# Cached keys turned in 32x32 squares: both attentions of the sample rows laid out anew

## The chip, the cores and the metric

One Trainium2 chip, one of its cores. The metric is the device time of one execution in microseconds. The engines that matter below: TensorE (PE; its weight load is shown apart as PEld), VectorE (DVE), ScalarE (ACT), GpSimd (POOL) and SyncE (SP), whose queue issues nearly all transfers between the chip's memory and the on-chip memory.

## The reference

One decoder layer runs over 512 prompt rows and over 32 sample rows (8 sequences of 4 new rows), all in fp32. The layer mixes an mLSTM and a differential attention, then attends to 256 memory tokens, then runs a gated feed-forward network. Only two parts for the sample rows matter here.

Differential attention over a paged cache: 8 sequences, 2 pages of 128 rows each, 4 heads, each head with two components of 64 numbers:

```python
past_k = cache_dk[l][page_table].reshape(Bs, past_len, DA_HEADS, 2, DA_QK_DIM)
s = einsum('bqhcd,bkhcd->bhcqk', q, k) * DA_QK_DIM ** -0.5   # k: 256 cached rows and the 4 new ones
p = softmax(where(mask, s, -inf))
a = p[:, :, 0] - lam * p[:, :, 1]
out = einsum('bhqk,bkhd->bqhd', a, v)
```

Attention to cached memory tokens: 8 sequences, 256 tokens, 4 heads of 256 numbers:

```python
s = einsum('bqhd,bkhd->bhqk', q, mk) * MEM_HEAD_DIM ** -0.5
o = einsum('bhqk,bkhd->bqhd', softmax(s), mv)
```

The keys of both caches lie in memory with the rows (tokens) outermost, while a score is a sum over the numbers of a head; so the keys have to be turned before TensorE, which sums over partitions, can use them.

## The kernel before

The program is one long function; instructions are recorded in program order, and a planner then orders them on each engine by simulated times and priorities. On each engine that order is fixed when the kernel runs. `burst` and `issue_after` keep groups of matmuls together. On-chip memory is divided into rings of tiles: six staging tiles of 1024 columns (`stage()`), four weight slots of 2048 (`wp`), eleven larger tiles (`S`), and banks of the accumulation memory (`mmp()`, five; `at()`, three). A tile's next use waits until its last user is done. Weights arrive in a staging tile, and Scalar and Vector split them into a high and a low part in a weight slot; three matmuls then make one fp32 product.

Paged attention (the loop over `pipe(NB, dk_load, dk_turn, dk_scores)`): `dk_load` gathers the two pages of a sequence into one staging tile, 128 rows on 128 partitions. `dk_turn` transposes each head's 128x128 square on TensorE (`tr`, L1225), and Scalar and Vector copy the results out of the accumulation memory into a weight slot (`kT`, L1226); GpSimd adds the four new rows (L1221). `dk_scores` multiplies them per head with queries in which the other component is zero (`qz`, L1238), two sequences at a time. Vector masks and takes the maximum, Scalar the exponential and its sum, for each sequence apart (`sample_exp`, L1055 and L1056). `sample_softmax` then scales, by matmuls with selecting coefficients (`csz`, L1075), so that both components are combined and all sequences stand in one tile, which two transposes and eight copies spread for the product with the values. In each step of this loop one step of the prompt's own attention (`next(prompt)`) and some leftover projections (`F.run`) are recorded, so that TensorE's work is mixed.

Memory attention: `mk_load` brings 128 tokens by 1024 numbers, `mk_turn` transposes eight squares on TensorE (L1476), copied out by Scalar and Vector (L1477); `mk_scores` does two matmuls for each head and sequence (L1484), then `sample_exp`; after all eight sequences `sample_softmax`, and `mv_out` sums the values (L1506). The loads begin before the second half of the query projection (`gemmB` over `hqT`, L485), the first four sequences are turned inside it, and the others between steps of the prompt's memory attention (`ch_soft`, `ch_turn`, `ch_out`). `mv_load` brings the values into staging tiles, weight slots and one S tile, as they come free. Output projection weights (`w_mo`) follow in the staging tiles.

Of the kernel before, what the change touches and what calls it, by code (L numbers as in the profile page):

```python
# [7 lines left out]
F32 = mybir.dt.float32  # L8
# [10 lines left out]
NB = 8  # L19
# [15 lines left out]
for _n, _w in (("ident", 128), ("cos", 40), ("sin", 40), ("nsin", 40), ("dmask", 8), ("cm4", 4), ("cA", 1), ("cB", 1),  # L35
               ("comb", 16), ("selD", 8), ("selX", 8), ("selB", 8), ("cmask", 128), ("maskT", 128), ("maskS", 32)):
    CONST_COLS[_n] = (_off, _w)
    _off += _w
# [39 lines left out]
def kernel(ctx: ExitStack, tc: tile.TileContext, I, O):  # L78
# [972 lines left out]
    csz = cst.tile([P, NB, NS], F32, name="csz")  # L1051
    nc.gpsimd.memset(csz, 0.0)

    def sample_exp(sall, b, ps, nm, su):
        VRED(out=nm[:, b:b + 1], in_=ps, axis=AX.X, op=MAX, negate=True)  # L1055
        ACT(out=sall[:, b, :], in_=ps, func=AF.Exp, bias=nm[:, b:b + 1], accum_out=su[:, b:b + 1])  # L1056

    def sample_softmax(sall, su, coef, sel, oname, between=None):


        cf = small(NB, "scf")
        nc.vector.reciprocal(out=cf, in_=su)
        if coef is not None:
            VTS(out=cf, in0=cf, scalar1=coef, scalar2=None, op0=MUL)
        VTT(out=cf, in0=cf, in1=sel, op=MUL)
        VTT(out=view(csz, 0, [(64, NB // 2), (48, 2), (1, 16)]),
            in0=con("comb").unsqueeze(1).unsqueeze(1).broadcast_to([P, NB // 2, 2, 16]),
            in1=cf.rearrange("p (i e) -> p i e", e=2).unsqueeze(3).broadcast_to([P, NB // 2, 2, 16]), op=MUL)
        az = S([P, 2, H, NB * NS], F32, oname + "z")
        nc.gpsimd.memset(az, 0.0)  # L1070
        w = sall.shape[2]
        pa = at("spa")
        for e in range(2):
            for i in range(NB // 2):
                mm(pa[NS * i:NS * i + NS, :w], lhsT=csz[:, 2 * i + e, :], rhs=sall[:, 2 * i + e, :], start=(e == 0), stop=(e == 1))  # L1075
        a = Z("spc")[:, :w]
        nc.scalar.copy(out=a, in_=pa[:, :w])
        behind = between() if between else None
# [8 lines left out]
        return a, [az[:, 0], az[:, 1]]  # L1087

    def gather(name, b, g, out):
        v = nc.sync.value_load(ptab[0:1, 2 * b + g:2 * b + g + 1], min_val=0, max_val=I[name].shape[1] - 1)  # L1090
        dma(out=out, in_=I[name][0, bass.ds(v, 1)].rearrange("n s h d -> (n s) (h d)"))
# [105 lines left out]
    qz = sm.tile([P, H, 2, 2, 16], F32, name="qz", tag="qz", bufs=1)  # L1197
    nc.gpsimd.memset(qz, 0.0)
    for c in range(2):
        rr = slice(64 * c, 64 * c + 64)  # L1200
        nc.gpsimd.tensor_copy(out=qz[rr, :, :, c, :], in_=dqT[rr, :, SEQ:].rearrange("p h (g r) -> p h g r", g=2))
# [9 lines left out]
    kst, kts, pts, aTs, outs, rcs = {}, {}, {}, {}, {}, {}  # L1211

    def dk_load(b):
        st = stage()
        kst[b] = [st[:, 0:512], st[:, 512:1024]]
        for g in range(2):
            gather("cache_dk", b, g, kst[b][g])

    def dk_turn(b):
        kt = kts[b] = wp.tile([P, H, 260], F32, name="kT", tag="W")  # L1220
        nc.gpsimd.tensor_copy(out=kt[:, :, 256:260], in_=dkT[:, :, SEQ + TS * b:SEQ + TS * (b + 1)])  # L1221
        for g in range(2):
            ps = at("tpk")
            for h in range(H):
                tr(ps[:, h * P:(h + 1) * P], kst[b][g][:, h * P:(h + 1) * P], ident)  # L1225
            (VCP if g else nc.scalar.copy)(out=kt[:, :, g * P:(g + 1) * P], in_=v2(ps, P))  # L1226

    def dk_scores(b):

        if b % 2 == 0:  # L1230
            return
        pair = {}
# [714 lines left out]
```

## Time and profile before

| | us |
|---|---|
| median of 3 runs | 949.08 |
| lowest, highest | 947.5, 950.35 |
| span of the profiled execution | 947.0 |

The profiled execution's own time is given by its span, from the first to the last instruction; the times of the runs lie some 0.5 to 3.4 us above it. The granted TensorE clock is full throughout (mean 0.995, lower only at the very end). The stretches named below: paged attention from about 245 to 286 us, memory attention from about 405 to 485 us of the span. The page gives busy time by engine; the stretches and the groups of instructions are answers to queries on the same trace. A row of the time line gives start and duration in us, engine, source line, operation and operands, and how many instructions are merged in it; a row of groups gives the form, the count, busy time, mean duration in ns, and the idle time of the engine before them.

### The profile page before, as it was taken

To read this page: it belongs to the slowest core of one execution; us is meant where nothing else is said; L and a number is where in the kernel's file an instruction comes from. 1 tells how busy PE (TensorE), PEld (TensorE's weight loads), DVE (VectorE), ACT (ScalarE), POOL (GpSimd) and SP (SyncE) were. 2 spreads that over 40 slices of the span, in tenths; PEclk is the share of its full clock that TensorE was granted. 3 is DMA by queue.
4 is the path that set the end of the run, shared out by engine and by line. 5 is a ranking of instruction groups with operands and counts; after the bars stand their busy time and mean duration, and the time that the engine had idled before them with its cause. 6 is when DMAs were issued, how large, how long until landed. Compare 5 with 4: busy or idle time off the path is not lost. (4 is left out here: it accounts for less than half of the span.)

```text
span 947.0 us, 17080 instructions
## 1 busy us (share of the span) xinstructions
PE 927.3 (98%) x6612; PEld 808.2 (85%) x6612; DVE 601.1 (63%) x1128; ACT 388.5 (41%) x750; POOL 195.9 (21%) x384
## 2 busy tenths in 40 slices
PE   8999999999999999999999999999999999999995
PEld 5899787889866778998777899989988998999974
DVE  6745145565887448735654778637757775676767
ACT  5655233344676457625544433322212222222232
POOL 6611000025432215300000554001110110110114
PEclk9999999999999999999999999999999999999998
DMA  8960023344870429946944732062043313512023
GB/s 273 301 197 7 1 89 137 89 123 139 270 265 7 165 97 340 297 155 211 358 167 135 209 122 80 26 179 67 17 133 108 94 27 96 149 49 90 24 92 117
DMA packets 120673, 130.27 MB, mean 138 GB/s; under 512 B 8567, under 2 KB 86232, under 8 KB 120592
## 3 DMA queue, kind: packets, MB, share of 16 engines
q1 hardware_dynamic: 114408, 125.69, 42.1%
q10 hardware_dynamic: 6184, 3.48, 1.2%
q8 instruction: 52, 0.85, 0.4%
q14 instruction: 29, 0.24, 0.1%
HBM read 112.22 MB, written 16.93 MB: 136 GB/s over the span
## 5 line engine op out<-in xcount | busy, mean ns | idle before, releaser
L485 PE MATMUL mm<-fT,wslot 128*128 128x256 f32 x1872 | 235.9, 288 | 0.0
L485 PEld LDWEIGHTS mm<-fT,wslot 128*128 128x128 f32 x1872 | 234.4, 188 | 1.8 <-issue 0.8
L146 ACT CAST wslot<-wst 128x1024 fp32r<-128x1024 f32 x125 | 130.8, 1050 | 251.3 <-issue 71.7
L147 DVE TENSOR_TENSOR wslot<-wst,wslot 128x1024 fp32r<-128x1024 f32 x125 | 155.1, 1245 | 81.3 <-ACT wslot L146 80.8
L1758 PE MATMUL mm<-wslot,act 128*128 128x512 f32 (+1 forms) x180 | 70.2, 391 | 0.0
L1759 PE MATMUL mm<-wslot,act 128*128 128x512 f32 (+1 forms) x180 | 70.0, 392 | 0.0
L1757 PE MATMUL mm<-wslot,act 128*128 128x512 f32 (+1 forms) x180 | 69.3, 387 | 0.0
L1663 POOL COPY cvo<-u 128x2 f32<-128x2 f32 x43 | 10.5, 243 | 203.6 <-DVE u L1661 193.5
L411 PE MATMUL mm<-wslot,hT 128*128 128x512 f32 x128 | 51.3, 402 | 0.0
L485 PE MATMUL mm<-hT,wslot 128*128 128x256 f32 (+1 forms) x384 | 51.0, 289 | 0.0
L413 PE MATMUL mm<-wslot,hT 128*128 128x512 f32 x128 | 51.0, 399 | 0.0
L412 PE MATMUL mm<-wslot,hT 128*128 128x512 f32 x128 | 50.8, 397 | 0.0
L1658 DVE TENSOR_TENSOR u<-mm,rsb 128x256 f32<-128x256 f32 x43 | 18.1, 424 | 50.0 <-PE mm L485 50.0
L485 PEld LDWEIGHTS mm<-hT,wslot 128*128 128x128 f32 x384 | 49.2, 188 | 0.5 <-issue 0.2
L1757 PEld LDWEIGHTS mm<-wslot,act 128*128 128x128 f32 x180 | 34.3, 191 | 8.0 <-issue 0.8
L1759 PEld LDWEIGHTS mm<-wslot,act 128*128 128x128 f32 x180 | 33.8, 188 | 7.3 <-issue 0.4
L1758 PEld LDWEIGHTS mm<-wslot,act 128*128 128x128 f32 x180 | 33.8, 188 | 7.2
L1675 ACT ACTIVATE c<-c 128x560 f32<-128x560 f32 x21 | 14.1, 672 | 56.7 <-DVE c L1669 56.7
L1669 DVE SCALAR_TENSOR_TENSOR c<-u,cvT,c 128x560 f32<-128x560 f32 x43 | 34.3, 797 | 0.9
L1668 DVE SCALAR_TENSOR_TENSOR c<-u,cvT,c 128x560 f32<-128x560 f32 x43 | 34.1, 793 | 0.2
L1770 DVE TENSOR_TENSOR yp<-mm,yp 128x512 f32<-128x512 f32 (+1 forms) x41 | 27.2, 673 | 5.2 <-PE mm L1759 5.1
L413 PEld LDWEIGHTS mm<-wslot,hT 128*128 128x128 f32 x128 | 24.1, 188 | 5.0
(476 smaller groups left out, 1850.8 us busy)
## 6 DMA issues: line engine op xcount, KB each, us to landing
wst<-in_w_up_dram SPq DMA_DIRECT2D x42, 512.0 KB
wst<-in_w_in_dram SPq DMA_DIRECT2D x28, 512.0 KB
wst<-in_w_down_dram SPq DMA_DIRECT2D x20, 512.0 KB
wst<-in_cache_mem_k_dram SPq DMA_DIRECT2D x16, 512.0 KB
vt<-in_cache_mem_v_dram SPq DMA_DIRECT2D x10, 512.0 KB
wst<-in_w_mk_dram SPq DMA_DIRECT2D x8, 512.0 KB
xb<-in_x_prompt_dram SPq DMA_DIRECT2D x8, 512.0 KB
wst<-in_cache_dk_dram SPq DMA_DIRECT2D x16, 256.0 KB
```

The lines of the kernel that those rows point to most:

```text
L146: nc.scalar.copy(out=hi, in_=src)
L147: (eng or nc.vector).tensor_tensor(out=lo, in0=src, in1=f32(hi), op=SUB)
L411: mm(ps[b], lhsT=xt.hi(k, c0, c0 + n), rhs=s[:, 0, kk, :], start=(k == 0), stop=False)
L412: mm(ps[b], lhsT=xt.hi(k, c0, c0 + n), rhs=s[:, 1, kk, :], start=False, stop=False)
L413: return mm(ps[b], lhsT=xt.lo(k, c0, c0 + n), rhs=s[:, 0, kk, :], start=False, stop=(k == nk - 1))
L485: mm(ps[i], lhsT=s[:, l, k, :], rhs=x(k, c0, c1), start=(k == 0 and j == 0), stop=(k == 7 and j == 2))
L1668: STT(out=c, in0=u[:, 1:EXT - 1], scalar=w[1], in1=c, op0=MUL, op1=ADD)
L1669: STT(out=c, in0=u[:, 0:EXT - 2], scalar=w[0], in1=c, op0=MUL, op1=ADD)
L1757: mm(ps, lhsT=t[:, 0, c0:c0 + P], rhs=s[:, 0, i % 2, cs], start=st, stop=False)
L1758: mm(ps, lhsT=t[:, 0, c0:c0 + P], rhs=s[:, 1, i % 2, cs], start=False, stop=False)
L1759: return mm(ps, lhsT=t[:, 1, c0:c0 + P], rhs=s[:, 0, i % 2, cs], start=False, stop=en)
L1770: VTT(out=y, in0=ps, in1=y, op=ADD)
```

## The change

The keys' way is rebuilt in both attentions.

Layout. A load now takes one head: 32 partitions hold tokens t = 0..31 of four runs of 32 tokens, and the four heads fill the 128 partitions. So each page (paged) or half of the memory tokens is fetched by four loads instead of one, with rows of 512 bytes (paged) or 1 KB (memory). Vector then turns the whole tile in place in 32x32 squares; after it a partition holds head h and number d mod 32, and the free dimension tokens. TensorE's transposes and the copies out of the accumulation memory are gone.

Scores. Queries are spread by GpSimd into a block-diagonal tile (`qx`), so one matmul sums over 32 numbers of all four heads at once for two sequences' queries; four (paged) or eight (memory) pieces of a head are needed. In the paged part the four pieces land in four groups of 32 result rows; in the memory part pieces are accumulated in pairs. Scalar copies the raw scores to `sc`. Matmuls with 0/1 selections (`selK`, `selE`) then sum the groups and gather the sequences, and one softmax runs over 4 sequences at a time (paged, two tiles) or over all 8 (memory). The paged new rows get sixteen small matmuls of their own (`dk_new`).

Placement. In the memory part two sequences come together in the order 0, 2, 4, 6, 1, 3, 5, 7: three in staging tiles, one in an S tile, four in weight slots as the projection releases them; values reuse the same places. The constants that are loaded at the start grow by 168 columns.

```diff
-        for g in range(2):
-            gather("cache_dk", b, g, kst[b][g])
+        for g in range(2):
+            src = page("cache_dk", b, g)
+            for h in range(H):
+                dma(out=v2(st[NS * h:NS * h + NS, 512 * g:512 * g + 512], P),
+                    in_=src[:, :, h].rearrange("n (k t) d -> t (n k) d", t=NS))
     def dk_turn(b):
...
-                tr(ps[:, h * P:(h + 1) * P], kst[b][g][:, h * P:(h + 1) * P], ident)
-            (VCP if g else nc.scalar.copy)(out=kt[:, :, g * P:(g + 1) * P], in_=v2(ps, P))
+        nc.vector.transpose(out=kst[b], in_=kst[b])
+    for h in range(H):
+        for j in range(4):
+            r, f = slice(NS * j, NS * j + NS), slice(NS * h, NS * h + NS)
+            nc.gpsimd.tensor_copy(out=qx[f, j, :, TS * h:TS * h + TS], in_=v2(dqT[r, h, SEQ:], TS))
+            nc.gpsimd.tensor_copy(out=kn[f, j, :], in_=dkT[r, h, SEQ:])
...
         for c in (b, b - 1):
+            ps = mmp("ssc")[:, :256]
+            kv = kst[c].rearrange("p (k j t) -> p k j t", j=4, t=NS)
+            for j in range(4):
                 with burst(t):
+                    t = mm(v2(ps[NS * j:NS * j + NS], NS), lhsT=pair(c, j), rhs=kv[:, :, j, :], start=True, stop=True).ins
+            nc.scalar.copy(out=sc[:, c, 0:256], in_=ps)
+    def dk_sum():
+                    t = mm(pS[e][i:i + NS], lhsT=con("selK")[:, NS * (b % 2):NS * (b % 2) + NS], rhs=sc[:, b], start=True, stop=True).ins
+    def da_softmax(between):
+        for e in range(2):
+            VTT(out=pS[e][:, 256:260], in0=pS[e][:, 256:260], in1=con("cm4"), op=ADD)
+            VRED(out=nm[:, e:e + 1], in_=pS[e], axis=AX.X, op=MAX, negate=True)
+            ACT(out=p[:, e], in_=pS[e], func=AF.Exp, bias=nm[:, e:e + 1], accum_out=su[:, e:e + 1])
+        for e in range(2):
+            VTS(out=cs[:, e], in0=con("comb"), scalar1=cf[:, e:e + 1], scalar2=cv, op0=MUL, op1=MUL)
+        for e in range(2):
+            mm(pa[64 * e:64 * e + 64], lhsT=cs[:, e], rhs=p[:, e], start=True, stop=True)
...
+    def mk_load(b):
+        kst[b] = two(home[b])
         for c in range(2):
             for h in range(H):
+                dma(out=v2(kst[b][c][NS * h:NS * h + NS], 256),
+                    in_=I["cache_mem_k"][0, b, c * P:(c + 1) * P, h].rearrange("(k t) d -> t k d", t=NS))
+    def mk_turn(b):
+        for t in kst[b]:
+            nc.vector.transpose(out=t, in_=t)
+    def mk_scores(bs):
+                for j in range(8):
+                    g = NS * (j % 4)
+                        t = mm(v2(ps[g:g + NS, c * P:c * P + P], NS), lhsT=qx[:, j, b // 2 * 2:b // 2 * 2 + 2].rearrange("p n r -> p (n r)"),
+                               rhs=kv[:, :, j, :], start=(j < 4), stop=(j >= 4)).ins
+            nc.scalar.copy(out=sc[:, b], in_=ps)
+    for k in range(4):
+        mk_load(SEQS[k])
     for i, _ in enumerate(gemmB(hqT, [ev_q(m) for m in range(4, 8)])):
+        if i % 4 == 1:
+            mk_turn(SEQS[i // 4])
         if i % 4 == 3:
+            mk_load(SEQS[4 + i // 4])
     next(prompt)
     next(prompt)
+    mk_scores(SEQS[:4])
+    for k in range(3):
+        mv_load(SEQS[k])
+    mv_load(SEQS[3])
+    for k in range(4, 8):
+        mk_turn(SEQS[k])
     next(prompt)
+    t = mk_scores(SEQS[4:])
+    for k in range(4, 8):
+        mv_load(SEQS[k])
     next(prompt)
+    mk_sum(t)
```

More of the change, by code (lines that the diff above doesn't have):

```diff
@@ L1294 @@
     prompt = pipe(4 * H, da_soft, lambda i: None, da_turn, da_av, da_end)
[L1295 to L1296 removed]
+    sc = S([P, NB, 260], F32, "sc")
     for t, _ in enumerate(pipe(NB, dk_load, dk_turn, dk_scores)):
@@ L1307, in step @@
         return summed[0].ins
-    aw, az = sample_softmax(sall, su, cv, con("selD"), "da", step)
+    pS = [at("pS")[:, :260] for _ in range(2)]
+    dk_sum()
+    aw, az = da_softmax(step)
     F.run(4)
```

185 lines of the change are left out of this document (86 added, 99 removed).

## The prediction

> **What bounds the kernel now.** I read the page first (who is busy), then the stretches of the two cached-row attentions, then the order of instructions on TensorE and on the issuing queue inside them. On the page TensorE is busy nearly throughout:
>
> ```profile
> span 947.0 us, 17080 instructions
> PE 927.3 (98%) x6612; PEld 808.2 (85%) x6612; DVE 601.1 (63%) x1128; ACT 388.5 (41%) x750; POOL 195.9 (21%) x384
> ```
>
> The stretches (columns: window, its length, busy time of PE, PEld, DVE, ACT, POOL with instruction counts, granted clock, DMA share, GB/s). The second is the paged attention, the third the stretch from the second half of the query projection over the memory attention up to the output projection, the fourth its part up to the last key scores:
>
> ```profile
> 220.00:245.00 25.00, 25.00 (x258) 23.48 (x257) 15.70 (x45) 10.60 (x26) 15.89 (x23) 1.00 0.37 117
> 245.00:286.50 41.50, 38.33 (x309) 27.76 (x307) 37.05 (x109) 33.70 (x116) 15.70 (x20) 1.00 0.78 260
> 404.80:485.20 80.40, 80.34 (x772) 69.47 (x771) 43.43 (x93) 39.59 (x114) 1.81 (x1) 1.00 0.71 250
> 404.80:456.20 51.40, 51.34 (x490) 46.64 (x488) 22.41 (x47) 20.77 (x58) 1.81 (x1) 1.00 0.62 204
> ```
>
> They differ. In the memory stage TensorE has no gap (80.34 of 80.40) and Vector is about half busy: work taken from TensorE there should come off the time. In the paged stage TensorE (38.33 of 41.50) and Vector (37.05) are both nearly full.
>
> **The change, part by part.** *Memory stage, TensorE.* 128 full transposes go; the score matmuls become twice as many at half the width, 256 instructions instead of 128 (each fp32 matmul is two in the trace). TensorE's order of work, start and duration first:
>
> ```profile
> 410.83 1.47 PE L1476 MATMUL tpk<-cpk,wst 128*128 128x128 f32 x12
> 412.06 2.49 PE L485 MATMUL mm<-hqT,wslot 128*128 128x256 f32 x18
> 414.39 0.60 PE L1476 MATMUL tpk<-cpk,wst 128*128 128x128 f32 x4
> 414.74 4.00 PE L485 MATMUL mm<-hqT,wslot 128*128 128x256 f32 x30
> ...
> 434.10 1.47 PE L1476 MATMUL tpk<-cpk,wst 128*128 128x128 f32 x12
> ...
> 447.61 5.09 PE L1476 MATMUL tpk<-cpk,wst 128*128 128x128 f32 x40
> 452.63 3.66 PE L1484 MATMUL ssc<-kT,qs 128*32 128x256 f32 x64
> 456.22 0.65 PE L1445 MATMUL cpt<-cpk,cp 128*128 128x128 f32 x4
> ...
> 286.57 1.95 PE L1337 MATMUL ops<-vt,daz 128*32 128x128 f32 x64
> 288.46 0.71 PE L1281 MATMUL oda<-dvN,aT 128*128 128x128 f32 x4
> ```
>
> Start to start, 40 transposes take 5.02 us, 126 ns each; in the short groups between the projection's matmuls it is 103 and 88 (1.23/12, 0.35/4), so some 110 on average and 128 x 0.110 = 14.1 us go. The old scores cost 3.59/64 = 56 ns, 7.2 us in all. The new shape, 32 columns of queries against 128 columns, stands there already as the weighted sum of paged values: 1.89/64 = 29.5 ns, so 256 cost 7.6 us. The eight summing matmuls replace eight combining ones of the same shape. Net -13.7. The keys are now read in runs of 32 with steps between, which no row shows: at no extra cost the price is 29.5 ns; at worst that of a 256-wide one, 56, which would cost 6.8 us. I take the first, as its row has the same columns and size.
>
> *Memory stage, Vector and Scalar.* Evictions and per-sequence softmax go, sixteen in-place turns of 128x1024 come:
>
> ```profile
> L1477 DVE COPY kT<-tpk 128x512 f32<-128x512 f32 x16 | 11.0, 686 | 9.0 <-PE tpk L1476 9.0
> L1055 DVE TENSOR_REDUCE snm<-ssc 128x1 f32<-128x256 f32 x8 | 3.4, 425 | 2.4 <-PE ssc L1484 2.4
> L147 DVE TENSOR_TENSOR wslot<-wst,wslot 128x1024 fp32r<-128x1024 f32 x8 | 9.7, 1226 | 6.4 <-ACT wslot L146 6.2
> L1226 DVE COPY kT<-tpk 128x512 f32<-128x512 f32 x8 | 5.4, 675 | 0.2 <-PE tpk L1225 0.2
> L1226 ACT COPY kT<-tpk 128x512 f32<-128x512 f32 x8 | 4.8, 604 | 0.6 <-PE tpk L1225 0.6
> ```
>
> No Vector turn stands in the trace. From below: two of the 675 ns copies have half its elements each, and a turn would hardly be under one of them (0.68). From above: twice the 1226 ns of the same size with two inputs (2.45). I take 1.23, the row of the same size. Vector: 43.4 - 11.0 - 3.4 - 0.7 + 16 x 1.23 + 0.9 = 48.9 us, in a stage that shrinks to 66.7. It fits, but the last eight turns (9.8 us) stand among the prompt's softmax steps, and the transposes that filled TensorE's waits for those are gone. For that I give back 2 us. Scalar loses more than it gets.
>
> *GpSimd* spreads queries: sixteen small copies by some 0.2 us and a memset, where it is busy 1.81 of 80.4; nothing. In the paged part there are 32 copies and a memset; near are
>
> ```profile
> 197.99 0.66 POOL L958 COPY qzm<-qT 128x32 f32<-128x32 f32 x4
> 231.27 6.06 POOL L942 TENSOR_TENSOR vz<-vS,cpk 128x512 fp32r<-128x512 f32 x6
> ```
>
> so 32 x 0.165 = 5.3 us plus 0.5. Their tile takes a weight slot, free only when the output gate's projection lets one go. GpSimd has 9.1 us idle from 220 to 245, and behind the copies wait the masked values (L942) for the state update: cover enough, and if not, up to 5.8 us later state stores, which free the staging tiles of the paged keys.
>
> *Transfers.* Paged keys go from 16 loads to 64 of 64 KB in 512-byte rows; memory keys from 16 to 64 of 128 KB in 1 KB rows; each lands on 32 partitions. The issuing queue shows the price of an issue:
>
> ```profile
> 246.03 2.28 SPq L1091 DMA_DIRECT2D wst<-in_cache_dk_dram  x4
> 249.55 4.18 SPq L1091 DMA_DIRECT2D wst<-in_cache_dk_dram  x6
> 265.96 4.11 SPq L1091 DMA_DIRECT2D vt<-in_cache_dv_dram  x8
> 393.36 29.74 SPq L1467 DMA_DIRECT2D wst<-in_cache_mem_k_dram  x10
> ```
>
> A paged load with its page lookup takes 4.11/8 = 0.51 us, so a page of four at most 2.05 and sixteen pages 33 us of issue instead of 8. Staging tiles come free as now: from 246 twelve pages need 25 us, to 271, landing about 273. The last key transposes now run at 269.59 (the row stands below). The values' loads, behind them on that queue, start some 5 us later than 266 and no longer wait for slots held by turned keys.
>
> For the rate, three rows of transfers: a lone 128 KB load on 32 partitions, the query weights in 512-byte rows, the memory values in 4 KB rows (the last two 128 partitions wide):
>
> ```profile
> 289.50:292.50 3.00, 3.00 (x40) 1.56 (x38) 3.00 (x4) 1.32 (x4) 0.00 (x0) 1.00 0.17 44
> 391.00:395.00 4.00, 4.00 (x33) 4.00 (x33) 3.31 (x5) 1.86 (x4) 2.89 (x2) 1.00 1.16 303
> 459.00:465.00 6.00, 6.00 (x50) 4.72 (x48) 3.90 (x9) 3.38 (x10) 0.00 (x0) 1.00 1.02 410
> ```
>
> GB/s over share gives what the 16 engines move when busy: 259, 261 and 402. Both effects multiplied give the floor, 259 x 261/402 = 168; the ceiling is 402; I take 259, for the partitions are certain and 1 KB rows lie between. The memory keys (64 x 131 KB, 8.39 MB) then need 32 us, now 21. Four sequences load from about 397 (first issue 393.36, with the engines still full of query weights at 395) and are there by 413; the other four wait for a weight slot each, the last freed where the projection ends: now 434.10, less three times 1.57 us of transposes inside it, about 430. It lands near 436, is turned by 439, and TensorE comes to the last scores at 456.2 - 13.7 = 442.5. Behind the keys go 8.39 MB of memory values, 21 us: from 434 with the last keys to about 459; the second half of the value sum, now 19 us after the last scores, comes at 462:
>
> ```profile
> 475.55 4.52 PE L1506 MATMUL pso<-vt,caz 128*32 128x256 f32 x80
> ```
>
> Three microseconds of room in both; for slips of the two I give back 0.3.
>
> The Trainium skill, SBUF — State Buffer, section on the DMA port swizzle, says that 32 partitions reach 8 of the 16 ports, with an asymptote of 218 GB/s. The lone load's 259 against 402 bears that out in kind. By 218 as an estimate the last keys land 0.7 us later, and the sum below would be 0.7 us higher.
>
> *Paged stage.* TensorE loses 64 transposes and gains little:
>
> ```profile
> 269.59 1.04 PE L1225 MATMUL tpk<-cpk,wst 128*128 128x128 f32 x8
> 270.46 0.61 PE L1281 MATMUL oda<-dvN,aT 128*128 128x128 f32 x4
> 221.81 0.44 PE L841 MATMUL mls<-qT,kT 128*32 128x32 f32 x8
> 222.18 0.61 PE L948 MATMUL mlks<-cpk,kT 128*32 128x128 f32 x4
> ```
>
> At (270.46 - 269.59)/8 = 109 ns, 119 with the groups of four, 64 x 0.119 = 7.6 us go; 32 instructions for the new rows at (222.18 - 221.81)/8 = 46 ns add 1.5, the sums 1.0, the two wider combining matmuls save 0.6: -5.7. Vector loses eight evictions (5.4), eight maxima (3.4), and about 2.0 of masks and coefficients, and gets eight turns (9.8) and 2.0 for the joint softmax: 38.0 instead of 37.05. So the stage can give at most 41.5 - 38.0 = 3.5, and the later keys take that or more: bounds -3.5 and +6, taken 0.
>
> *Start.* The constants grow by 168 columns (86 KB, ahead of the first transposes; 0.3 us at 279 GB/s): +0.3.
>
> ```profile
> 0.00:25.00 25.00, 21.42 (x90) 14.13 (x90) 14.93 (x18) 13.91 (x21) 16.09 (x26) 1.00 0.87 279
> ```
>
> **Sum.** -13.7 + 2 + 0.3 + 0 + 0.3 = -11.1 on the profiled 947.0, so 935.9. The median shown is 949.08, 2.1 above that span, so I say 938.
>
> **Rivals.** (a) *The paged keys come late.* Each issue as dear as in the six at 249.55 (0.70 us) makes twelve pages 33 us, keys at 281 and the last scores some 10 us later than now; TensorE's order is fixed, so the prompt's work cannot move ahead, and the stage ends 7 to 10 us later. For it: those six issues; against: they stood among stores, and the eight at 265.96 went faster. Time: 945 to 948.
>
> (b) *Everything is taken*: no softmax exposure, and the paged stage gives its 3.5: 949.1 - 13.7 - 3.5 + 0.3, about 932.
>
> (c) *Slower: the memory keys are too slow.* Place: the last scores, for which TensorE waits in order. They ran at 456 before; from 397 that leaves 59 us, less 2.5 for two turns. Below 8.39/57 = 147 GB/s, or 0.89 us per piece, the change loses. At 120 GB/s the keys land at 467, scores end near 471, 15 us late: about 963. For it: 32 partitions, rows a quarter as long, four times the pieces, all at once; against: even the product of both effects is 168, and eight loads of 256 KB issued 0.51 us apart filled the engines:
>
> ```profile
> 270.00:275.00 5.00, 5.00 (x42) 3.30 (x41) 4.39 (x14) 4.40 (x15) 3.27 (x2) 1.00 1.05 374
> ```
>
> The Trainium skill, SBUF — State Buffer, section on the setup-cost knee, gives a transfer about 2 us beside its bytes; one after the other 64 pieces would by that estimate take some 147 us. The row just shown speaks against their standing one after the other.
>
> (d) *Vector becomes the bound.* At t per turn the memory stage needs 29.2 + 16t and the paged 28.2 + 8t of Vector. At 2.45 these are 68.4 and 47.8: -12.0 and +6.3, about 944. The whole is lost from about t = 2.7, above my bound. Against it: the quoted row of this size, with two inputs, takes half of 2.45.
>
> (e) *No change*: the stage is as long for another reason, such as memory values that arrive as late as now, when they fill the engines (share 1.02 at 459 to 465), because their tiles come free no sooner. Then 949.
>
> **How the numbers follow.** Forecast 0.48, (a) 0.14, (b) 0.08, (d) 0.06, (e) 0.08, (c) 0.16. A difference of 0.3% is 2.8 us, about what a measurement tells from no change; 0.05 of (a) ends inside it. Faster 0.48 + 0.09 + 0.08 + 0.06 = 0.71, same 0.08 + 0.05 = 0.13, slower 0.16. The likeliest's own range is 931 to 943. The range for 8 in 10 takes in (b) and (a), (e) and the near end of (c): 928 to 954.
>
> **What would show it.** In the profile after: no TensorE transposes before the scores; turns of some 1.2 us (over 2: d); the memory stage 66 to 70 us instead of 80.4 with TensorE still above 95%; waits of TensorE or Vector for the memory key load near nothing (many us: c); the paged stage between 38 and 48 us, with its last scores near 270 (280 or more: a). I am wrong if TensorE's gaps in the memory stage grow by as much as its work shrinks.

## The result, and the profile after

The changed kernel is slower. Its median is 962.62 us (962.46 to 963.65, four runs); the kernel before, beside it, has 949.23 us. The ratio is 1.0139, with a 95% interval of 1.0126 to 1.0153: 13.4 us more. I had said 938.

The page after, its first lines (span, then busy time of each engine, its share of the span, and instructions):

```profile
span 960.9 us, 17244 instructions
PE 918.8 (96%) x6584; PEld 798.7 (83%) x6584; DVE 602.7 (63%) x1108; ACT 373.1 (39%) x715; POOL 206.7 (22%) x422
```

TensorE is busy 8.5 us less than before (927.3), as the change meant, and the span is 13.9 us longer: TensorE's idle time went from 19.7 us (947.0 - 927.3) to 42.1. The stretches: the paged attention and the whole memory stage, cut at the same instructions as the second and third row of before, and the first part of the memory stage, the projection's second half, for which the row of before stands under it (window, length, busy time of PE, PEld, DVE, ACT, POOL, granted clock, DMA share, GB/s):

```profile
244.40:294.36 49.96, 37.38 (x284) 23.87 (x282) 38.52 (x105) 29.68 (x104) 15.38 (x17) 0.93 0.72 229
412.60:496.00 83.40, 70.77 (x771) 62.18 (x770) 51.79 (x88) 29.46 (x93) 5.48 (x17) 0.93 0.85 252
412.60:444.60 32.00, 27.02 (x196) 26.61 (x195) 21.84 (x25) 4.43 (x15) 2.75 (x12) 0.89 0.89 194
```
```profile
404.80:434.30 29.50, 29.50 (x244) 29.50 (x243) 7.69 (x14) 7.48 (x19) 1.81 (x1) 1.00 0.49 155
```

The paged stage is 50.0 us long instead of 41.5. The memory stage is 83.4 instead of 80.4, although TensorE works 70.8 us in it instead of 80.3; its first part takes 32.0 instead of 29.5, with 196 matmuls in it instead of 244. In both stages the clock is no longer full. By the ends of the stages, 7.8 of the 13.9 us are there when the paged stage ends and 10.8 when the memory stage ends (496.0 instead of 485.2); the rest, some 3 us, comes behind it, most of it because the clock stays at half until 500.9.

**Paged stage.** Vector, TensorE and the issuing queue in the time line (start, duration, operation; in brackets the idle time before and what ended it):

```profile
254.22 1.25 DVE L1224 STREAM_TRANSPOSE wst<-wst 128x1024 f32<-128x1024 f32 x1 [3.08 <-DMA wst<-in_cache_dk_dram]
```
```profile
256.45 0.45 PE L1291 MATMUL tpa<-cpk,pda 128*128 128x128 f32 x1 [4.99 <-DVE pda L1283]
...
273.40 0.41 PE L1291 MATMUL tpa<-cpk,pda 128*128 128x128 f32 x2 [2.27 <-DVE rc L1281]
...
277.34 1.07 PE L1251 MATMUL ssc<-wst,wx 128*32 128x256 f32 x16
...
294.36 1.96 PE L1360 MATMUL ops<-vt,daz 128*32 128x128 f32 x64
```
```profile
253.67 20.19 SPq L1220 DMA_DIRECT2D wst<-in_cache_dk_dram  x38
```

Vector stands 3.1 us before a turn whose keys have not come. Behind the turn, on the same engine, stands the prompt's `pda` (L1283), and for that TensorE stands 5.0 us. The last scores run at 277.3 (before: 272.7), the value sum begins at 294.4 (before: 286.6).

**Projection.** Scalar's and Vector's waits from 404 to 446, as totals (engine and line, for whom, us, times, longest), and the row of TensorE:

```profile
ACT qs L1442 <- DVE ql L1440: 25.4, 7, 8.7
DVE wst L1517 <- DMA wst<-in_cache_mem_k_dram: 11.4, 5, 7.4
DVE kvt L1517 <- DMA kvt<-in_cache_mem_k_dram: 5.5, 5, 1.5
```
```profile
424.11 20.43 PE L485 MATMUL mm<-hqT,wslot 128*128 128x288 f32 x143 [3.84 <-ACT qs L1442]
```

Vector stands 16.9 us before turns of memory keys, and behind them wait the projection's own evictions, the copies of its results out of the accumulation memory (`ql`, L1440), for these Scalar (`qs`), for Scalar TensorE.

**End of the memory stage.** The output projection's weights, the issue, and then Scalar and TensorE:

```profile
481.80 3.06 SPq L231 DMA_DIRECT2D wst<-in_w_mo_dram  x6
```
```profile
488.59 2.19 ACT L146 CAST wslot<-wst 128x1024 fp32r<-128x1024 f32 x2 [8.69 <-issue]
```
```profile
492.47 0.69 PE L1614 MATMUL ost<-cpk,oS 128*128 128x128 f32 x2 [6.11 <-ACT oS L1611]
```

Before, these weights were issued at 471.2, as the first part of the value sum (from 470.5) let go of their tiles. Now that part runs from 473.2 to 476.0 and they go out at 481.8, since 24 small loads of the convolution state (L1626 to L1628) stand ahead of them on the queue. Scalar stands before the weights' cast, with the copy `oS` behind it.

**The clock.** The windows in which the granted clock (the third number from the end) is not full:

```profile
255.00:260.00 5.00, 3.55 (x55) 2.34 (x55) 4.53 (x12) 2.42 (x7) 1.10 (x1) 0.52 0.46 130
260.00:265.00 5.00, 4.75 (x38) 3.28 (x34) 3.47 (x10) 3.57 (x15) 4.33 (x5) 0.80 0.49 133
...
420.00:425.00 5.00, 1.16 (x5) 0.96 (x6) 4.61 (x6) 1.25 (x3) 0.80 (x4) 0.74 0.47 123
425.00:430.00 5.00, 5.00 (x26) 5.00 (x26) 3.16 (x5) 0.75 (x3) 0.92 (x4) 0.58 1.05 229
...
490.00:495.00 5.00, 2.09 (x10) 1.72 (x10) 4.80 (x5) 4.68 (x9) 0.00 (x0) 0.57 1.00 385
495.00:500.00 5.00, 5.00 (x12) 3.77 (x13) 4.33 (x17) 1.08 (x4) 0.00 (x0) 0.50 0.02 10
500.00:505.00 5.00, 5.00 (x21) 3.79 (x20) 0.18 (x1) 0.00 (x0) 0.00 (x0) 0.91 0.02 3
```

After each of the three long gaps TensorE works at about half speed for 5 to 9 us. Busy time times the missing share of the clock, summed over these rows, is 1.7 + 0.9 + 0.3 + 2.1 + 0.9 + 2.5 + 0.5 = 8.9 us, an estimate, since a row mixes stretches at full and at half clock. So the account, as far as this estimate holds, is: TensorE's work at full clock shrank by some 17.4 us (8.5 + 8.9), slow clock took 8.9 back, and gaps 22.4.

### The profile page after: what moved, and what is told of

Its sections match the earlier page's. It is cut to its first block, busy times and chain, and to the rows that moved or that the text cites. A ratio compares the mean times of both kernels' runs of the same rounds, so it can differ in the third digit from the quotient of the medians.

```text
span 960.9 us, 17244 instructions
## 1 busy us (share of the span) xinstructions
PE 918.8 (96%) x6584; PEld 798.7 (83%) x6584; DVE 602.7 (63%) x1108; ACT 373.1 (39%) x715; POOL 206.7 (22%) x422
## 5 line engine op out<-in xcount | busy, mean ns | idle before, releaser
L146 ACT CAST wslot<-wst 128x1024 fp32r<-128x1024 f32 x125 | 130.7, 1049 | 261.3 <-issue 80.4
L485 PE MATMUL mm<-hqT,wslot 128*128 128x256 f32 x192 | 27.0, 305 | 5.0 <-ACT qs L1442 5.0
L485 PEld LDWEIGHTS mm<-hqT,wslot 128*128 128x128 f32 x192 | 26.4, 204 | 5.4 <-ACT qs L1442 5.4
```

The costliest lines, as they stand in the source:

```text
L146: nc.scalar.copy(out=hi, in_=src)
L485: mm(ps[i], lhsT=s[:, l, k, :], rhs=x(k, c0, c1), start=(k == 0 and j == 0), stop=(k == 7 and j == 2))
```

## The experiments

The edits are made on the changed kernel unless said otherwise. The orders on the engines are planned anew for each kernel, so a variant can also differ from it where it was not edited. Times are medians, ratios are against the kernel before in the same session (948.2 to 949.6 us), with 95% intervals.

### One part alone

The paged part alone (the memory part and its softmax taken from the kernel before):

```diff
-            mk_turn(SEQS[i // 4])
+                mk_turn(j)
...
-        az = mem_softmax()
+        _, az = sample_softmax(sall, su, None, con("selX"), "ca")
```

> Only the paged attention is changed, the memory attention is that of before. In the trace of the changed kernel the paged stage ended 7.8 us later than before and the memory stage lost another 6. If the two losses are independent, this is 949.2 + 7.8 = 957. Rival: the delay of the paged stage is absorbed by later slack (values, output gate) and the loss is the memory stage's alone: 949 to 951.

The memory part alone (the paged part taken from the kernel before):

```diff
-    wx = wp.tile([P, 640], F32, name="wx", tag="W")
+    qz = sm.tile([P, H, 2, 2, 16], F32, name="qz", tag="qz", bufs=1)
...
-    dk_sum()
-    aw, az = da_softmax(step)
+    aw, az = sample_softmax(sall, su, cv, con("selD"), "da", step)
```

> Only the memory attention is changed, the paged one is that of before. Independent losses: 962.6 - 7.8 = 955. If this part would have given what I forecast but for the paged part (rival): 938 to 940.

Measured: 959.1 (1.0099, 1.0076 to 1.0123) and 954.0 (1.0050, 1.0035 to 1.0065). The two losses are 9.5 and 4.4 us and add up to 13.9; both together cost 13.4. So within these intervals they add up and nothing shows that one hides the other. Both parts lose, and the gain I forecast for the memory part does not come even where the paged part is untouched.

### Arrival of the keys, or order

Without the turns:

```diff
-        nc.vector.transpose(out=kst[b], in_=kst[b])
+        pass
...
-            nc.vector.transpose(out=t, in_=t)
+            pass
```

> The changed kernel without its 24 in-place turns on Vector (the scores are then taken from unturned keys; all else is computed). Loads, matmuls and softmax stay. Theory A, the harm is that Vector, which works in order, stands before a turn whose keys are not there, with the evictions of the projection and the prompt's softmax behind it: these go on now, the projection's second half loses its 7.8 us and the paged stage some 5, so 949 to 952. Theory B, the keys come too late for TensorE itself, whoever turns them: TensorE then waits at the scores, 958 to 963. The 30 us of Vector work that go are not on the path in either.

Measured: 957.0 (1.0082, 1.0055 to 1.0109), between the two theories. The projection's second half, as a window of this run:

```profile
411.05:435.20 24.15, 24.15 (x196) 24.15 (x195) 3.83 (x8) 4.24 (x13) 1.84 (x8) 1.00 1.08 211
```

It takes 24.2 us instead of 32.0, without a gap, though the narrow loads are the same and carry 211 GB/s at a full share (the changed kernel: 198 to 229 where its share is full): there theory A holds. But the paged stage hardly gains (the value sum begins at 292.8 instead of 294.4), and the output weights stay late: TensorE stands 5.3 us before `ost`, and 4.8 us before the second part of the value sum, whose memory values come late.

The keys loaded wide:

```diff
-            for h in range(H):
-                dma(out=v2(kst[b][c][NS * h:NS * h + NS], 256), in_=...[0, b, c * P:(c + 1) * P, h]...)
+            dma(out=kst[b][c], in_=...[0, b, c * P:(c + 1) * P].rearrange("t h d -> t (h d)"))
```

> The changed kernel, but each key tile is loaded as before the change, whole rows on 128 partitions in one load (16 loads of 256 KB and 16 of 512 KB instead of 64 and 64 pieces). The tiles then hold the keys in another order, so the sample rows' scores are computed from mixed-up keys; all work on the engines is the same. Theory A (the cost lies in how the keys arrive: 32 partitions at half rate, four issues for one): the last paged scores go back from 278 to some 272, the projection's second half loses its stall of 8 us, and only the joint softmax (some 3 us in the paged stage) and the late output weights (some 6 us) stay: 941 to 947. Theory B (it lies in where the turns and small loads were put, whatever the rate): 955 to 962.

Measured: 952.5 (1.0050, 1.0032 to 1.0068), off both forecasts, because the two stages went opposite ways. The memory stage, from the projection's second half to the output projection, and then the paged stage's TensorE and issuing queue:

```profile
418.40:488.75 70.35, 67.24 (x771) 59.38 (x770) 47.88 (x86) 29.52 (x94) 5.48 (x17) 0.98 0.79 279
```
```profile
258.87 0.45 PE L1288 MATMUL tpa<-cpk,pda 128*128 128x128 f32 x1 [7.02 <-DVE pda L1280]
...
300.16 1.95 PE L1357 MATMUL ops<-vt,daz 128*32 128x128 f32 x64
```
```profile
258.00 5.87 SPq L1218 DMA_DIRECT2D wst<-in_cache_dk_dram  x6
```

The memory stage is 13 us shorter (70.4 instead of 83.4), with the turns still where the planner puts them. Not all of it is the keys: the output weights also go out earlier here, 1.3 us after their tiles are free, and the gap before `ost` is 2.4 us instead of 6.1. Vector still stands 10.7 us before turns in the projection, but late enough in it that TensorE runs through (24.1 us). In the paged stage wide loads give nothing: its end is 5.8 us later than in the changed kernel, with the clock at half for 20.5 us from 251.1 on. The last six loads (0.98 us each instead of 0.36) wait for staging tiles, and Vector stands before the turns again. So in the paged stage the 32 partitions and the count of issues cannot be the whole cause, since the loss stays without them.

The same pieces on all 128 partitions, one run of 32 tokens of all heads at a time (the memory loads; the paged ones are cut likewise):

```diff
-            for h in range(H):
-                dma(out=v2(kst[b][c][NS * h:NS * h + NS], 256), in_=...h].rearrange("(k t) d -> t k d", t=NS))
+            for k in range(4):
+                dma(out=kst[b][c][:, 256 * k:256 * k + 256], in_=...[c * P + NS * k:...].rearrange("t h d -> h t d"))
```

> The changed kernel with each group of four loads cut otherwise: not one head on 32 partitions with four runs of tokens, but one run of 32 tokens of all four heads on 128 partitions. Same bytes, same pieces (64 KB and 128 KB), same row lengths, same count of issues; the tile that results is the same. Theory A (32 partitions halve the rate, some 200 GB/s at full share): the memory keys come in 26 us or less instead of 40, the projection's second half no longer stalls, 7.8 us come back, and the paged keys, which one issue per 0.5 us limits to 130 GB/s, come no sooner: 952 to 956. Theory C (the rate is set by the number of pieces and their rows): as after, 961 to 964.

Measured: 1028.3 (1.0833, 1.0805 to 1.0861). Both theories missed. A window in the middle of the key loads, and their issue:

```profile
450.00:460.00 10.00, 2.72 (x12) 2.72 (x13) 5.37 (x6) 0.30 (x3) 0.00 (x0) 0.50 0.27 92
```
```profile
467.11 22.79 SPq L1512 DMA_DIRECT2D kvt<-in_cache_mem_k_dram  x16
```

With nothing else to move, the engines are busy 27% and carry 92 GB/s: as much as four or five of the sixteen would. The Trainium skill, DMA: Bandwidth & Descriptors, section Why a DMA increments its semaphore by 16 and not by 1, says that a load is spread over the largest number of engines, at most 16, that divides the slowest dimension of both sides; here that is the four heads. The trace agrees: it has four 4-byte packets beside the data of each load (28 for seven loads from 450 to 460), one for each engine by that section, and the changed kernel has 16 to 17 for each. The run therefore says nothing on partitions; read with that page, it shows that the outermost dimension of these loads set how many engines carried them.

### The order at the end, and the place of the turns

The small loads behind the output weights:

```diff
-    for g in range(6):
-        conv_in(cr, 20 * g, 0, ...)
+    with tc.issue_after(loaded[0]):      # the last w_mo load so far
+        for g in range(6):
+            conv_in(cr, 20 * g, 0, ...)
```

> The changed kernel with one edit of order: the 24 small loads of the convolution state are queued on the issuing queue behind the first output-projection weights, not ahead of them. In the trace of the changed kernel these weights were issued at 481.8, 5.8 us after the tiles they need had been read; TensorE then stood 6.1 us. If that is a loss of its own: 962.6 - 5 to 6.5 = 956 to 957.5. Rival, the weights would be late by the transfers anyway, or the small loads are then late for the convolution: 961 to 964.

Measured: 955.6 (1.0086, 1.0065 to 1.0106), 7.0 us less, just below the forecast: a loss of its own. This run's paged stage, in which nothing was edited, shows something else. TensorE's row and a window of this run, then the same window of the changed kernel:

```profile
274.13 0.66 PE L1293 MATMUL tpa<-cpk,pda 128*128 128x128 f32 x2 [2.64 <-DVE rc L1283]
```
```profile
275.00:280.00 5.00, 5.00 (x18) 3.58 (x17) 2.74 (x5) 2.85 (x9) 0.05 (x1) 0.50 0.89 277
```
```profile
275.00:280.00 5.00, 5.00 (x48) 2.82 (x46) 4.45 (x12) 4.14 (x15) 2.82 (x2) 1.00 0.91 277
```

The same gap is 2.64 us here and 2.27 there; here the clock is halved behind it, and the value sum begins at 298.1 instead of 294.4. The row itself starts 0.7 us later, the value sum 3.8: the slow clock costs 3 us.

The first eight memory turns behind the projection's evictions, then both edits of order on the memory part alone:

```diff
-        if i % 4 == 1:
-            mk_turn(SEQS[i // 4])
+    with tc.issue_after(lastql[0]):
+        for k in range(4):
+            mk_turn(SEQS[k])
```

> The changed kernel with the first eight turns of the memory keys queued on Vector behind the last eviction of the query projection instead of among its evictions. Theory A (Vector standing before a turn holds up the projection): the projection's second half goes from 31.8 to some 24 us; 10 us of turns then stand ahead of the prompt's softmax, of which TensorE sees some 4: 957 to 960. Theory B (the keys are late for TensorE itself): what the projection gains is waited for at the scores, 961 to 964.

> Only the memory attention is changed, the paged one is that of before, and both edits of order are made: the output weights ahead of the small loads, the first eight turns behind the projection's evictions. From 954.0 of the memory part alone: 5.5 less for the weights and 1 to 4 less for the turns, 944 to 947, under the 949 of before. If the two losses overlap or the keys are late for TensorE itself: 948 to 952.

Measured: 959.5 (1.0118, 1.0098 to 1.0138) and 951.4 (1.0033, 1.0019 to 1.0047). The first is where theory A had it. The second missed its forecast and lies in its rival's range, for another reason than the rival's: with the first eight turns gone, the planner put turns of the later sequences into the projection, and Vector stood before these up to 9.2 us. So all sixteen went behind the projection, and the small loads to GpSimd's queue:

```diff
+    with tc.issue_after(lastql[0]):
+        for k in range(4, 8):
+            mk_turn(SEQS[k])
-        conv_in(cr, ...)
+        conv_in(cr, ..., nc.gpsimd.dma_start)
```

> Only the memory attention is changed, with all sixteen turns queued on Vector behind the projection's last eviction, and the 24 small loads of the convolution state on GpSimd's queue, out of the way of the output weights. In the kernel with the first eight turns behind (951.4) Vector still stood 9.2 us before a turn of the second four inside the projection, TensorE lost 3.6 us there, and 2.6 us more for the small loads behind the weights. If these are the whole loss: 951.4 - 6 = 945, below before. If the keys are late for TensorE itself: 949 to 952.

Measured: 950.6 (1.0019, 1.0008 to 1.0030): in the range of the second case, but not for its reason. The projection runs through, but TensorE then stands 6.6 and 5.0 us. Two of its rows:

```profile
437.18 5.44 PE L1524 MATMUL ssc<-wst,qx 128*32 128x128 f32 x95 [6.61 <-POOL qx L1422]
...
448.62 1.08 PE L1473 MATMUL cpt<-cpk,cp 128*128 128x128 f32 x4 [5.02 <-DVE cp L1464]
```

The second is the prompt's softmax behind sixteen turns in a row. The first I took for the turns too; it is GpSimd's spread of the queries, behind the small loads that I had put on that queue.

### The paged stage

The spread on Vector:

```diff
-            nc.gpsimd.tensor_copy(out=qx[f, j, :, TS * h:TS * h + TS], in_=v2(dqT[r, h, SEQ:], TS))
-            nc.gpsimd.tensor_copy(out=kn[f, j, :], in_=dkT[r, h, SEQ:])
+            VCP(out=qx[f, j, :, TS * h:TS * h + TS], in_=v2(dqT[r, h, SEQ:], TS))
+            VCP(out=kn[f, j, :], in_=dkT[r, h, SEQ:])
```

> The changed kernel with the 32 spreading copies of the paged part on Vector instead of GpSimd. Theory A: these copies (5.5 us on GpSimd, 220 to 232) stand ahead of the masked values there, the state update starts 3.5 us later (238.6 instead of 235.1), its stores, the staging tiles and with them the paged keys come as much later; on Vector, idle then, they cost nothing and 3 to 4.5 us come back: 958 to 959.5. Rival: the keys are held by their own issue (0.53 us a piece, 34 us) and by the staging tiles, which are now kept until the scores: 961 to 964.

The turn and the scores one step later:

```diff
-    for t, _ in enumerate(pipe(NB, dk_load, dk_turn, dk_scores)):
+    for t, _ in enumerate(pipe(NB, dk_load, lambda b: None, dk_turn, dk_scores)):
```

> The changed kernel with the turn and the scores of the paged keys one step of the pipeline later behind their loads. Theory A (Vector stands before keys that are not there yet, with the prompt's softmax behind): the gap of 5 us at 251 goes, and the halved clock behind it: 956 to 959. Theory B (the keys come when they come; a later step puts the last scores and the joint softmax later): 962 to 967.

The spread on GpSimd, but behind the masked values:

```diff
+            with tc.issue_after(masked[0]):      # the last L942
                 nc.gpsimd.tensor_copy(out=qx[f, j, :, TS * h:TS * h + TS], in_=v2(dqT[r, h, SEQ:], TS))
                 nc.gpsimd.tensor_copy(out=kn[f, j, :], in_=dkT[r, h, SEQ:])
```

> The changed kernel with the 32 spreading copies of the paged part queued on GpSimd behind the masked values of the state update. Theory A: the update starts 3.5 us sooner, and with it its stores, the staging tiles, the keys: 958 to 959.5. Theory B (in the kernel with the copies on Vector, an engine waiting in order was only replaced by another; the keys are late by their issue): 961 to 965.

Measured: 967.3 (1.0193, 1.0176 to 1.0210), slower than both forecasts; 963.1 (1.0141, 1.0124 to 1.0158), which is theory B; and 959.3 (1.0117, 1.0103 to 1.0132). On Vector the copies took 0.295 us each and stood in front of a product for which TensorE then waited 3.0 us: the load moved, the wait came along. The lag left the gap (4.77 us instead of 4.99). Behind the masked values the theory held. GpSimd's row of these values in this run, then in the changed kernel:

```profile
230.90 6.05 POOL L943 TENSOR_TENSOR vz<-vS,cpk 128x512 fp32r<-128x512 f32 x6
```
```profile
235.47 6.05 POOL L942 TENSOR_TENSOR vz<-vS,cpk 128x512 fp32r<-128x512 f32 x6
```

They start 4.6 us sooner (before the change: 231.27), the last 38 key loads go out at 250.5 instead of 253.7, the value sum begins at 292.0 instead of 294.4, and 3.3 us come back. The gap before the first `tpa` stays (4.3 us), and with it most of this stage's loss: why the first paged keys come too late for Vector's order, with wide loads as with narrow ones, is not settled. One candidate stands in the changed kernel's trace: the third sequence's loads stand on the issuing queue from 245.7 to about 252 among four state stores (L1010), each of which waits for Vector (8.5 us in all), and its turn is the one that Vector waits for at 254.2; before the change that sequence's two loads went out together at 240.3. No run changed that order. Fewer staging tiles in use at once, or an order on Vector that puts the prompt's softmax ahead of the turns, was not tried either.

### The turns where the keys are

On the memory part alone: two turns behind the second pair of evictions, then four, four and six:

```diff
+    for k, p in enumerate((6, 4, 4, 2, 2, 0, 0, 0)):
+        with tc.issue_after(qls[-1 - p]):
+            mk_turn(SEQS[k])
```

> Only the memory attention is changed; small loads on GpSimd's queue; the turns placed by the trace of the kernel with late turns: two behind the second pair of evictions of the projection (410.9), four behind the next (416.8), four behind the one after (422.9), six behind the last (428.8), in pauses of Vector of 5.2 us each. Theory A (only the places were wrong; all keys but the last two sequences have landed by then): the waits of TensorE at 437 (6.6 us) and 449 (5.0 us) go for the most part, 950.6 - 6 to 10 = 941 to 945. Theory B (the rate): Vector stands before keys again, 948 to 952.

Measured: 943.7 (0.9952, 0.9940 to 0.9964): theory A, at the same key loads. What is left is TensorE's wait for the spread behind the small loads:

```profile
434.92 5.98 PE L1524 MATMUL ssc<-wst,qx 128*32 128x128 f32 x95 [4.92 <-POOL qx L1422]
```

The small loads behind the spread, and then, in a further kernel, the last four turns behind the prompt's first two softmax steps:

```diff
+    with tc.issue_after(spread[0]):
         for g in range(6):
             conv_in(cr, ..., nc.gpsimd.dma_start)
```
```diff
-    for k, p in enumerate((6, 4, 4, 2, 2, 0, 0, 0)):
+    for k, p in enumerate((6, 4, 4, 2, 2, 0)):
...
+    with tc.issue_after(softs[0]):
+        for k in (6, 7):
+            mk_turn(SEQS[k])
```

> Only the memory attention is changed, turns placed between the evictions as in the kernel of 943.7, and the small loads on GpSimd's queue behind the spread of the queries. That kernel's gap of 4.9 us before the first scores goes: 943.7 - 4 to 6 = 938 to 940, which is the 11 us below before that my sum gave for this part alone. Rival: the first scores then wait for something else (turns of the last sequences, whose keys landed at 439): 941 to 944.

> The best kernel so far (942.9, only the memory attention changed) with the turns of the last two sequences queued on Vector behind the prompt's first two softmax steps. There TensorE stood 8.1 us for a softmax row that stood on Vector behind four turns, each waiting for keys. If the order is the cause, the gap shrinks to 1 to 3 us and the last scores come at about 446 instead of 449: 938 to 940. If the rate is (last keys at 440, turned by 442 either way), TensorE only waits at the last scores instead: 942 to 944.

Measured: 942.9 (0.9941, 0.9922 to 0.9961) and 939.7 (0.9920, 0.9905 to 0.9935). The first is the rival: its gap went and another of 8.1 us opened behind turns that waited for keys. Moving four turns closed that too. The memory stage of the last kernel, Vector's turns between two pairs of evictions, and TensorE's one wait for a turn:

```profile
402.96:474.50 71.54, 67.83 (x771) 59.70 (x769) 48.13 (x84) 28.83 (x91) 16.88 (x37) 0.98 1.03 290
```
```profile
415.45 0.76 DVE L1437 SCALAR_TENSOR_TENSOR ql<-mm,qh 128x256 fp32r<-128x256 f32 x2 [2.95 <-ACT qh L1436]
416.12 4.61 DVE L1516 STREAM_TRANSPOSE wst<-wst 128x1024 f32<-128x1024 f32 x4
421.50 0.76 DVE L1437 SCALAR_TENSOR_TENSOR ql<-mm,qh 128x256 fp32r<-128x256 f32 x2 [0.76 <-ACT qh L1436]
```
```profile
440.74 0.64 PE L1528 MATMUL ssc<-kvt,qx 128*32 128x128 f32 x16 [1.95 <-DVE kvt L1516]
```

71.5 us instead of 80.4 before the change. This kernel, the change of the memory part alone with four edits of order, is 8.5 us faster than the one before. Last, the whole change with these orders (without that last move of four turns) and the spread behind the masked values:

```diff
+            with tc.issue_after(masked[0]):          # paged spread
+        with tc.issue_after(qls[-1 - p]):            # memory turns
+    with tc.issue_after(spread[0]):                  # small loads
```

> The whole change with all orders mended: paged spread behind the masked values, memory turns placed, small loads out of the way. If the parts add up, the kernel above plus what the paged part still loses with its spread mended (its stage ended at 292.0, before 286.6: 5.4 us): 943 to 946. If the paged part's rest is absorbed later: 938 to 941.

Measured: 948.8 (0.9999, 0.9984 to 1.0013), above both forecasts. Its trace still has gaps of 4.4 and 3.3 us in the paged stage, and one of 6.2 us behind turns in the memory stage. By the runs with one part each (9.5 us of loss less the 3.3 that the order of the spread gave back) the paged part still costs about the 6 us that the memory part gives; the paged part mended alone was not run.

## Why the prediction was wrong

**TensorE's work: right.** Transposes go, the scores are cheap. The group of the turns, and the row of the new scores:

```profile
L1224 DVE STREAM_TRANSPOSE wst<-wst 128x1024 f32<-128x1024 f32 x8 | 9.9, 1244 | 11.0 <-DMA wst<-in_cache_dk_dram 8.0 <-DMA nrow<-in_state_ml_n_dram 3.0
```
```profile
454.99 3.70 PE L1529 MATMUL ssc<-kvt,qx 128*32 128x128 f32 x128
```

128 score matmuls take 3.63 us to the next instruction, 28 ns each (I took 29.5), so reading the keys in runs of 32 costs nothing. TensorE's work shrank by some 17.4 us; I had 13.7 + 5.7. A turn takes 1.244 us, I took 1.23; rival (d) falls.

**The step that failed: who waits for the keys.** I asked only when TensorE would come to the last memory scores (442.5) and found the keys turned by 439. The turns are instructions on Vector, which works in order, and behind a turn without keys stand the evictions of the projection and the prompt's softmax. I looked at that for TensorE's order, not for Vector's, and so put these waits at nothing. The runs show the loss of the memory stage there: Vector stood 16.9 us before turns, and the projection's second half took 32.0 us, but 24.2 with the same loads and no turn. On the memory part alone, moving only the turns, at the same loads, took the time from 950.6 to 943.7; with all the edits of order the stage is 71.5 us, which comes near the 66 to 70 that I forecast. (My 442.5 was the end of the last scores, not their start: 456.2, from which I took it, is where the old ones end. They would begin at about 439, so the three microseconds of room were not there; in the last kernel 1.95 us of wait are left at that place.)

**The rate: mis-sized, and the trigger.** I took 259 GB/s at a full share; from 425 to 430 it was 229 at 1.05, and 211 at 1.08 without turns. The Trainium skill's 218 (SBUF — State Buffer, section on the DMA port swizzle) was the better number. By it I reckoned 0.7 us, because I asked about the last key only; the first eight tiles, due by 413, were turned from 413.2 to 430.6, all within the projection. From 405 to 425 the keys came slower still, at 123 to 196 GB/s with a share down to 0.47: the issuing queue itself stood, 4.4 us of it for `ql` on Vector, which came late behind the turns, and the sixteen loads from 414.9 on took 12.2 us to issue; without turns the same sixteen took 8.6.

**The 2 us given back for the prompt's softmax behind turns:** the place was right in two of the variants (gaps of 8.1 and 5.0 us), the size was not; the changed kernel itself has no such gap.

**GpSimd's spread "nothing": wrong.** The copies took 0.203 and 0.279 us on average instead of 0.165, 7.7 us in all instead of 5.3, and the cover of 9.1 us of idle time was no cover, because the masked values stood behind them in order: 4.2 us later, and 3.3 us of the kernel's time. I had named the condition (up to 5.8 us later stores) and priced it at zero.

**Paged stage: 0 taken, +8.5 measured,** outside my bounds of -3.5 and +6. The issue price held (20.19/38 = 0.53 us, I took 0.51), but "staging tiles come free as now" did not: the stores that free them came later, and the last keys were turned at 275.9; I had them landing at about 273, and yet the last scores near 270; these ran at 277.3. Rival (a) had the place of the loss and its sign, and with 7 to 10 us its size; as a cause its dear issues do not suffice, as the wide loads show. What did delay these keys is only shown in part (the spread, 3.3 us); the rest stays open.

**The output weights: not in the sum at all.** Loads that the change does not touch (the convolution state) came to stand ahead of them: 7.0 us.

**Rival (c)** named 963 at 120 GB/s, break-even 147. The time was hit by luck, the mechanism was not: the memory keys came at some 180 GB/s on average (8.39 MB from 402 to 448), above that break-even, TensorE did not wait for keys at the last scores, and the loss sat in the projection, at the output weights and in the paged stage. My closing condition, that I am wrong if TensorE's gaps in the memory stage grow by as much as its work shrinks, came true and more: its work there fell by 9.6 us, and its gaps grew from 0.06 us to 12.6 (83.40 - 70.77).

## What to carry to other kernels

When work moves to an engine that executes in order, find for each moved instruction when its data arrive and what is queued behind it on that engine; the price of a late transfer is paid there first, not where the result is used. In the memory stage the slower transfer by itself cost this kernel little (1.95 us of wait for a key are left): with the same loads, moving turns and small loads behind the right instructions made a loss of 4.4 us a gain of 8.5. And a gap of some two microseconds or more on TensorE is to be priced with the slow clock that can follow it.

## What the runs showed of the hardware

The clock. In these traces TensorE's granted clock is full or half, and it changes in steps: each stretch at half clock lasts a whole multiple of 3.41 us (6.83, 6.83 and 10.24 in the changed kernel). Whether a gap brings it depends less on the length of the gap than on how busy TensorE is in the step. With the spread behind the masked values a gap of 2.24 us falls mostly into one step (busy 1.44 of 3.41 us, 42%), and the next step stands at half clock:

```profile
441.23:444.64 3.41, 1.44 (x13) 1.23 (x11) 2.51 (x5) 0.20 (x1) 0.02 (x1) 1.00 0.75 226
444.64:448.06 3.42, 3.15 (x50) 2.82 (x54) 3.21 (x8) 2.20 (x9) 2.72 (x5) 0.50 0.55 96
```

In the memory part alone a longer gap, 2.94 us, is shared by two steps (busy 60% and 54%), and the clock stays full:

```profile
434.76:438.17 3.41, 2.03 (x18) 1.82 (x16) 2.15 (x2) 0.32 (x2) 0.00 (x0) 1.00 0.62 161
438.17:441.59 3.42, 1.86 (x42) 1.40 (x46) 3.37 (x7) 2.00 (x9) 1.91 (x5) 1.00 0.80 186
441.59:445.00 3.41, 3.41 (x103) 3.21 (x94) 2.74 (x6) 1.72 (x7) 0.82 (x1) 1.00 0.74 251
```

In all the traces of this case, without their first 20 us, 60 gaps of TensorE are longer than 2 us. Behind 55 of them the clock was halved; behind those of 2.17, 2.27, 2.34, 2.46 and 2.94 us it was not. Of the steps at full clock in which TensorE was busy for less than 46%, 53 of 55 were followed by a step at half clock; of those from 46 to 56%, 6 of 20; of the busier ones, 3 of some 4700. The Trainium skill, TensorE: Matmul & The Clock Gate, section What's actually happening, gives half the clock after one or more idle windows of about 3.4 us, and says that the window runs on by itself. The half and the length of the step agree with these rows; but the step need not be idle throughout, since 42% busy was little enough. In the changed kernel the slow clock took some 8.9 us by the estimate above, beside 22.4 us of gaps.

The engines that carry a load: loads of 128 KB, cut with the four heads outermost, moved at 92 GB/s at a share of 0.27, with four 4-byte packets for each load; cut with 32 tokens outermost, at 198 to 229 GB/s at a full share (425 to 440), with 16 to 17.
